# A decoder layer in float32: the value projection by PSUM bank, a hand-written order at the FFN entry, a norm's last phase held back, evictions first

## The chip, the cores and the metric

The kernel runs on one core of a Trainium2 chip. The time is device microseconds of one execution, lower is better. Matmuls run on TensorE (PE in the profile, PEld its weight loads), elementwise work on VectorE (DVE) and ScalarE (ACT), a little on GpSimd (POOL). Weights come by DMA from the queue of SyncE (SP). Each engine takes its own instructions in the order of the program, and waits for the others by semaphores.

## The reference, cut to what matters

One layer (DEPTH 1) over 256 tokens of 2048 channels, in float32. The four parts that the text speaks of are here:

```python
h = rms_norm(x, norm_mix_pre)
proj = h @ w_in          # 2048 columns in, split into a_in, b_in, q, kv, nsa_g, merge_g
y_a = conformer_conv(a_in, ...)          # GLU, causal depthwise conv (31 taps), layer norm, silu, projection
y_b = chunked_spatial_gating(b_in, ...)
y_c = native_sparse_attention(q, kv, nsa_g, ...)
g_a, g_b, g_c = split(sigmoid(merge_g), 3)
mixed = (g_a * y_a + g_b * y_b + g_c * y_c) @ w_o
x = x + rms_norm(mixed, norm_mix_post)
h = rms_norm(x, norm_ffn_pre)
u = causal_depthwise_conv(h @ w_up, ffn_conv_w, ffn_conv_b)      # 3 taps
u_g, u_v = split(u, 2)
x = x + rms_norm((silu(u_g) * u_v) @ w_down, norm_ffn_post)
```

The 256 tokens are handled as two halves of 128 (`t` is 0 or 1). `w_up` has 2 x 5632 columns.

## The kernel before

**Split weights.** A float32 product is made of three matmuls on rounded parts: every operand is split into a high half (rounded to the format that PE multiplies) and a low half (what is left). A weight piece of 128 x 1024 is fetched into `wraw` (5 buffers) by `fetch` (L96), ACT copies it to `whi` (L136), DVE subtracts to get `wlo` (L137); `whi` and `wlo` have 4 buffers each. This is `piece()`. Activations are kept in pairs too: `hT` (mixer input) and `h2` (FFN input, `h2T` in the trace) hold for each of 16 chunks `k` of 128 channels a high and a low half.

There are two shapes of matmul. `mm_t` (L185 to L187) keeps the activation still and moves the weights, three matmuls per chunk and token half. `lumps` (L165, L172) keeps a weight chunk still and moves the activation: one matmul of high weights against both halves of the activation (L165, 512 columns for 256 tokens), and one of low weights against the high half (L172, 256 columns). Its order is high, low, high.

**Order.** The program is written in one order, and a scheduler at build time arranges each engine's instructions by priority and by its own estimate. `tc.high_priority(offset)` puts an instruction ahead in its choice, `tc.issue_after(ins)` pins it behind another. `in_line` does that for PE: a run of matmuls behind the run before. Work beside the matmuls is written as generators in a queue `bg`. `pump(ns)` takes from the front of that queue as much nominal work as its budget says; `until(mark)` empties it to a mark. The budgets are BA, BB, BC and BG for the four stages of the mixer, BG = 2000 per call for the gated branches.

**The mixer.** After the first projections the convolution's generators (`conv_gen`, L419, result `cv`) run on DVE beside the matmuls of the later projections. Behind them in the queue stands `lna_gen`, the layer norm of the convolution: sums and squares (`lnm`, `lnv`), two matmuls that sum over partitions (L426), a square root, and a last phase of eight steps that applies it (`lz`, `lg`, L453 to L459, result `At`). Then come the compressed attention and the attention proper.

**The value projection** (`pvs`, 560 columns: 256 values, 48 gate logits, 256 values) loops over the 16 chunks; a piece has all 560 columns of one chunk, and for each chunk four accumulators (two token halves x columns 0 to 304 and 304 to 560) get three matmuls each. After the loop six evictions on ACT (L624 to L626) write `kkv` and `gsg`. The pool of accumulators (`acc`) has four buffers, and the next tile (`ps`, the query projection) takes the first one that is evicted.

**The gates.** `branch` (three branches x four column blocks) computes the gate `pg`, its tanh in four evictions on ACT (L819, `mg`), the branch projection `py`, and their product on DVE (L842, L845). The evictions have no raised priority.

**The FFN entry.** The output projection `po` ends with its last blocks done half by half, so that half 0 is normed while PE computes half 1. `done_o(cb, t)` takes the square on ACT (L894), the product with the norm's weights (L900), and for the last block the norm `norm1` (L279, L280, the square root L221, L222 to L225) and four residual additions (L903, 512 channels each). `enter2(t, k)` transposes one chunk (L909, `ptf`, four buffers) and splits it into `h2` (ACT L915, DVE L916). The first two tiles of the up projection (`pu`) are computed half by half:

```python
for f in range(2):
    for n, run in enumerate(lumps(pu2[f], ws2[f], h2, 0)):
        in_line(run)
        c = 3 * f + n - 2
        for k in range(4 * c, 4 * c + 4) if c >= 0 else ():
            in_line(enter2, 1, k)
for f in range(2):
    for run in lumps(pu2[f], ws2[f], h2, 1):
        in_line(run)
```

With `t` given, the low run has 16 matmuls of 128 columns per tile and half. `order2` pins the two instructions of an `enter2` behind those of the one before; the other instructions of ACT and DVE there are placed by the scheduler. Behind follow the third tile, the sum of squares of the residual (L993, L996), its norm, and 85 more tiles of the up projection.

Of the kernel before, what the change touches and what calls it, by code (L numbers as in the profile page):

```python
# [29 lines left out]
FF = 5632  # L30
NFT = FF // 128
EPS = 1e-6
BA, BB, BC, BG = 3000, 3000, 2500, 2000
PR = 1000
NW0, _ = 9, 6
S1, S2, S3 = 6, 12, 14
# [11 lines left out]
def block(ctx: ExitStack, tc: tile.TileContext, x, fp, cst, rows, sgw, w1, w2, wf_a, wt_bv, wf_bu, wf_c,  # L48
# [130 lines left out]
    def in_line(work, *args):  # L179

        with tc.issue_after(pe_last[0]):
            pe_last[0] = work(*args)

    def mm_t(ps, xh, xl, hi, lo, first, last):
        PE.matmul(ps, lhsT=xh, rhs=hi, start=first, stop=False)  # L185
        PE.matmul(ps, lhsT=xh, rhs=lo, start=False, stop=False)  # L186
        return PE.matmul(ps, lhsT=xl, rhs=hi, start=False, stop=last).ins  # L187
# [235 lines left out]
    def lna_gen():  # L423
        def total(acc, nm):
            ps = bank([128, T], "lnp" + nm)
            PE.matmul(ps, lhsT=ones, rhs=acc, start=True, stop=True)  # L426
            return ps
        acc = q1("lnm")
        V.tensor_add(acc, ca[:, 0], ca[:, 1])
        yield 345  # L430
        for j in range(2, 8):
            V.tensor_add(acc, acc, ca[:, j])
            yield 345
        mean = total(acc, "m")
# [12 lines left out]
        V.tensor_scalar(var, total(acc, "v"), EPS, None, op0=ALU.add)  # L447
        r = rsqrt(P1, var, T, "a")
        yield 3400
        for j in range(8):  # L450
            z = q1(f"lz{j}")
            g = q1(f"lg{j}")
            V.tensor_mul(ca[:, j], ca[:, j], r)  # L453
            S.activation(z, ca[:, j], AF.Identity, bias=fps[:, C_LB + j:C_LB + j + 1],
                         scale=fps[:, C_LG + j:C_LG + j + 1])
            S.activation(g, z, AF.Tanh, scale=0.5)
            V.scalar_tensor_tensor(z, g, 1.0, z, op0=ALU.add, op1=ALU.mult)
            S.activation(At[:, j, 0], z, AF.Copy, scale=0.5)
# [148 lines left out]
    for i in range(4):  # L607
# [5 lines left out]

    pvs = [[PS.tile([128, 304 if b == 0 else 256], F32, tag="acc", name=f"pvs{t}{b}") for b in range(2)]
           for t in range(2)]
    for k in range(KT):
        hi, lo = piece(wt_vs[:, k * 560:k * 560 + 560], 560)
        for t in range(2):
            ts = slice(t * 128, t * 128 + 128)
            for b, c in ((0, slice(0, 304)), (1, slice(304, 560))):  # L620
                mm_t(pvs[t][b], hT[:, k, 0, ts], hT[:, k, 1, ts], hi[:, c], lo[:, c], k == 0, k == KT - 1)
        pump(BUDGET * .25)
    for t in range(2):
        S.activation(vsw[:, t, 0:256], pvs[t][0][:, 0:256], AF.Copy, scale=r0[:, t:t + 1])  # L624
        S.activation(gsg[:, t], pvs[t][0][:, 256:304], AF.Tanh, scale=rh[:, t:t + 1])  # L625
        S.activation(vsw[:, t, 256:512], pvs[t][1], AF.Copy, scale=r0[:, t:t + 1])  # L626
    gsgf = gsg.rearrange("p t c -> p (t c)")
    V.tensor_scalar(gsgf, gsgf, 1.0, 0.5, op0=ALU.add, op1=ALU.mult)

# [171 lines left out]
    def branch(bi, act_of):  # L801

        for cb in range(4):
# [12 lines left out]
            for t in range(2):  # L816
                for a in range(2):
                    tgs[t, a] = q1(f"mg{bi}{cb}{t}{a}")
                    S.activation(tgs[t, a], pg[t][:, a * 256:a * 256 + 256], AF.Tanh, scale=rh[:, t:t + 1])  # L819
# [18 lines left out]
            for t in range(2):  # L838
                for a in range(2):
                    cc = slice(cb * 512 + a * 256, cb * 512 + a * 256 + 256)  # L840
                    y = mac[:, t, cc] if bi == 0 else tgs[t, a]
                    V.scalar_tensor_tensor(y, tgs[t, a], 1.0, py[t][:, a * 256:a * 256 + 256], op0=ALU.add,  # L842
                                           op1=ALU.mult)
                    if bi:
                        V.tensor_add(mac[:, t, cc], mac[:, t, cc], y)  # L845
            if bi == 2:
                bg.append(mix_gen(cb))
            pump(BUDGET)
# [43 lines left out]
    def done_o(cb, t):  # L892
        cc = slice(cb * 512, cb * 512 + 512)
        S.activation(junk, po[cb, t], AF.Square, accum_out=ss1[t][:, cb:cb + 1])  # L894
        if cb < 3:
            V.tensor_mul(y1[:, t, cc], po[cb, t], rw[:, cc])
            return
        with tc.high_priority():
            r1 = norm1(ss1[t], f"o{t}")
            V.tensor_mul(y1[:, t, cc], po[cb, t], rw[:, cc])  # L900
            for c in range(4):
                cc = slice(c * 512, c * 512 + 512)
                V.scalar_tensor_tensor(y1[:, t, cc], y1[:, t, cc], r1, x2[:, t, cc], op0=ALU.mult, op1=ALU.add)  # L903

    def enter2(t, k):

        pt = bank([128, 128], f"ptf{t}{k}")
        ts = slice(t * 128, t * 128 + 128)
        tr = PE.transpose(pt, y1[:, t, k * 128:k * 128 + 128], ident)  # L909
        w = fps[:, C_NFP + k:C_NFP + k + 1]  # L910
        with ExitStack() as order:
            order.enter_context(tc.high_priority())
            for ins in order2:
                order.enter_context(tc.issue_after(ins))
            a = S.activation(h2[:, k, 0, ts], pt, AF.Copy, scale=w)  # L915
            v = V.scalar_tensor_tensor(h2[:, k, 1, ts], pt, w, h2[:, k, 0, ts].bitcast(F32), op0=ALU.mult,  # L916
                                       op1=ALU.subtract)
        order2[:] = [a.ins, v.ins]
        return tr.ins

    order2 = []
# [26 lines left out]
    for n, (cb, p) in enumerate(HELD):  # L948
        for i in range(2):
            if n == 0 and i == 0:  # L950
                pe_last[0] = mm_o(cb, 1, p, held[n], (i,))
            else:
                in_line(mm_o, cb, 1, p, held[n], (i,))
            if (n, i) == (3, 1):
                h2 = P0.tile([128, KT, 2, T], R, tag="hT", name="h2T")
            k = 2 * n + i - 7
            for k in ([k] if 0 <= k < 14 else [14, 15] if k == 14 else []):
                in_line(enter2, 0, k)
                if k % 4 == 3:
                    behind.append(tuple(order2))  # L960
                    up = wf_up[k // 8][:, k // 4 % 2 * 1024:k // 4 % 2 * 1024 + 1024]
                    ws2[k // 8].append(piece(up, 1024))
        if p == 7:
            done_o(cb, 1)
    P1c.close()


# [6 lines left out]
    pu2 = [PS.tile([128, 2, T], F32, tag="acc", name=f"pu{f}") for f in range(2)]  # L974
    for f in range(2):
        for n, run in enumerate(lumps(pu2[f], ws2[f], h2, 0)):
            in_line(run)
            c = 3 * f + n - 2
            for k in range(4 * c, 4 * c + 4) if c >= 0 else ():
                in_line(enter2, 1, k)  # L980
    for f in range(2):
        for run in lumps(pu2[f], ws2[f], h2, 1):
            in_line(run)
    with ExitStack() as order:
        order.enter_context(tc.high_priority())
        for ins in order2:
# [106 lines left out]
def _layout(inp):  # L1093
# [31 lines left out]
    wt_vs = c(w_in[:, vs_cols].reshape(16, 128, 560).transpose(1, 0, 2)).reshape(128, 16 * 560)  # L1125
# [72 lines left out]
```

## Time and profile before

| | |
|---|---|
| runs | 1608.62, 1609.54, 1611.83 us; median 1609.54 |
| profiled execution | 1607.9 us, span 1606.2 us |
| granted clock of PE | 0.997 |
| PE busy | 1586.2 us (99%), 8293 matmuls |
| DVE, ACT busy | 1125.6 us (70%), 855.0 us (53%) |
| read from HBM | 299.13 MB, 188 GB/s over the span |

A row of the timeline has the start and the duration in us, the engine, the line, the operation, output and inputs, the shape, the count of merged instructions, and in brackets the idle time ahead with what ended it. Matmuls are pipelined and the profile models their ends, so that what one costs is read from the distance of starts, not from its duration. A row of the waits has who waited at which line for whom: total us, times, longest.

### The profile page before, as it was taken

What the parts mean: (1) busy time and instruction counts of PE and PEld (TensorE: products, weight loads), DVE (VectorE), ACT (ScalarE), POOL (GpSimd) and SP (SyncE); (2) the same over time, 40 slices, a digit from 0 to 9 for tenths busy, and PEclk for the clock granted to TensorE, in tenths of its full rate; (3) what the DMA queues carried; (4) which work ended last, traced back from release to release, by engine and by line L of the source; (5) the groups of instructions that cost most, each with busy time, mean ns of one, the idle gap of its engine ahead of it and who ended that gap; (6) DMA issues with size and microseconds to landing.
All of it is one profiled execution on the core that took longest, in us unless ns stands there. A gap on an engine that the chain in (4) does not pass through costs nothing.

```text
span 1606.2 us, 22284 instructions
## 1 busy us (share of the span) xinstructions
PE 1586.2 (99%) x8293; PEld 1346.7 (84%) x8293; DVE 1125.6 (70%) x1914; ACT 855.0 (53%) x1378; POOL 16.1 (1%) x45
## 2 busy tenths in 40 slices
PE   9999998999999999999999999999999999999997
PEld 7888887888887777788888888888888888888886
DVE  6799999887655555555558877777777777444444
ACT  6554444475466766444455655555555555344342
POOL 0000020000000000000000000000000000000000
PEclk9999999999999999999999999999999999999999
DMA  8655556557655455566773566666666666666663
GB/s 304 228 193 184 185 158 198 180 182 241 209 160 151 141 164 175 179 188 189 242 237 96 192 189 191 186 189 192 192 187 185 192 189 213 196 194 195 194 191 114
DMA packets 85438, 303.74 MB, mean 189 GB/s; under 512 B 9809, under 2 KB 10193, under 8 KB 84689
## 3 DMA queue, kind: packets, MB, share of 16 engines
q1 hardware_dynamic: 84096, 298.04, 58.6%
q0 software_dynamic: 944, 4.19, 0.7%
q8 instruction: 65, 1.06, 0.3%
q14 instruction: 45, 0.36, 0.1%
q10 hardware_dynamic: 288, 0.08, 0.0%
HBM read 299.13 MB, written 2.10 MB: 188 GB/s over the span
## 4 chain that ended last, share of the span: by engine, by line
PE 96%; DVE 2%; issue 0%; DMA 0%; ACT 0%; SPq 0%; DVEq 0%; ACTq 0%
PE ps L165 28%; PE ps L172 15%; PE po L186 7%; PE po L187 7%; PE po L185 7%; PE pg L185 5%; PE pg L187 5%; PE pg L186 5%; PE py L186 3%; PE py L187 3%; PE py L185 3%; DVE cv L419 1%; PE pv L185 1%; PE pv L186 1%; PE pv L187 1%; PE s L685 1%
## 5 line engine op out<-in xcount | busy, mean ns | idle before, releaser
L137 DVE TENSOR_TENSOR wlo<-wraw,whi 128x1024 fp32r<-128x1024 f32 (+1 forms) x533 | 644.7, 1212 | 301.6 <-ACT whi L136 294.1
L136 ACT ACTIVATE whi<-wraw 128x1024 fp32r<-128x1024 f32 (+1 forms) x533 | 554.9, 1045 | 368.9 <-PE po L187 135.7
L165 PE MATMUL ps<-h2T,whi 128*128 128x512 f32 x1360 | 324.6, 391 | 0.0
L165 PEld LDWEIGHTS ps<-h2T,whi 128*128 128x128 f32 x1360 | 250.0, 188 | 48.3
L172 PEld LDWEIGHTS ps<-h2T,wlo 128*128 128x128 f32 x1360 | 174.4, 191 | 6.6
L172 PE MATMUL ps<-h2T,wlo 128*128 128x256 f32 x1360 | 176.7, 283 | 0.0
L165 PE MATMUL ps<-hT,whi 128*128 128x512 f32 x640 | 158.3, 395 | 3.9 <-ACT gsg L625 3.9
L187 PE MATMUL pg<-whi,hT 128*128 128x512 f32 x384 | 151.0, 393 | 0.0
L186 PE MATMUL pg<-wlo,hT 128*128 128x512 f32 x384 | 150.1, 391 | 0.0
L185 PE MATMUL pg<-whi,hT 128*128 128x512 f32 x384 | 148.8, 394 | 0.0
L207 ACT ACTIVATE t<-ps 128x256 f32<-128x256 f32 x125 | 47.5, 382 | 173.8 <-PE ps L165 173.7
L165 PEld LDWEIGHTS ps<-hT,whi 128*128 128x128 f32 x640 | 117.6, 190 | 26.1 <-ACT gsg L625 4.1
L185 PE MATMUL po<-whi,gh 128*128 128x512 f32 x336 | 130.7, 389 | 0.0
L186 PE MATMUL po<-wlo,gh 128*128 128x512 f32 x336 | 130.7, 389 | 0.0
L187 PE MATMUL po<-whi,gl 128*128 128x512 f32 x336 | 130.7, 389 | 0.0
L208 DVE TENSOR_TENSOR t<-ps,t 128x256 f32<-128x256 f32 x125 | 53.1, 426 | 91.2 <-ACT t L207 91.1
L419 DVE SCALAR_TENSOR_TENSOR cv<-hb,fps,cv 128x256 f32<-128x256 f32 x240 | 106.8, 493 | 0.8 <-ACT cv L415 0.7
L172 PEld LDWEIGHTS ps<-hT,wlo 128*128 128x128 f32 x640 | 84.1, 191 | 4.3
L172 PE MATMUL ps<-hT,wlo 128*128 128x256 f32 x640 | 85.9, 283 | 0.0
L187 PEld LDWEIGHTS pg<-whi,hT 128*128 128x128 f32 x384 | 72.1, 188 | 15.4 <-issue 0.7
L185 PEld LDWEIGHTS pg<-whi,hT 128*128 128x128 f32 x384 | 71.9, 188 | 15.5 <-issue 1.5
L186 PEld LDWEIGHTS pg<-wlo,hT 128*128 128x128 f32 x384 | 72.1, 188 | 15.0 <-issue 0.3
(297 smaller groups left out, 1900.5 us busy)
## 6 DMA issues: line engine op xcount, KB each, us to landing
wraw<-in_wf_up_dram SPq DMA_DIRECT2D x176, 512.0 KB, 4.3
wraw<-in_wt_g_dram SPq DMA_DIRECT2D x96, 512.0 KB, 3.8
wraw<-in_wt_dn_dram SPq DMA_DIRECT2D x88, 512.0 KB, 4.4
wraw<-in_wt_p_dram SPq DMA_DIRECT2D x48, 512.0 KB, 3.9
wraw<-in_wf_a_dram SPq DMA_DIRECT2D x32, 512.0 KB, 4.6
wraw<-in_wt_o_dram SPq DMA_DIRECT2D x32, 512.0 KB, 4.5
wraw<-in_wt_bv_dram SPq DMA_DIRECT2D x16, 512.0 KB, 6.4
wraw<-in_wf_bu_dram SPq DMA_DIRECT2D x16, 512.0 KB, 4.4
```

Source lines behind the costliest of these rows:

```text
L136: S.activation(hi[:, :n], raw[:, :n], AF.Copy)
L137: V.tensor_sub(lo[:, :n], raw[:, :n], hi[:, :n].bitcast(F32))
L165: ins = PE.matmul(ps[:, :, ts], lhsT=ws[k // 8][0][:, c:c + 128], rhs=mov[:, k, :, ts], start=(k == 0 and not t), stop=(k == n - 1), skip_ ...
L172: ins = PE.matmul(ps[:, 1, ts], lhsT=ws[k // 8][1][:, c:c + 128], rhs=mov[:, k, 0, ts], start=False, stop=False, skip_group_check=True).ins
L185: PE.matmul(ps, lhsT=xh, rhs=hi, start=first, stop=False)
L186: PE.matmul(ps, lhsT=xh, rhs=lo, start=False, stop=False)
L187: return PE.matmul(ps, lhsT=xl, rhs=hi, start=False, stop=last).ins
L207: S.activation(t1, ps[:, 1], AF.Copy)
L208: V.tensor_add(t1 if rb is not None else dst, ps[:, 0], t1)
L419: V.scalar_tensor_tensor(ca[:, j], hb[:, j, k:k + T], w(j, k), ca[:, j], op0=ALU.mult, op1=ALU.add)
L685: last = PE.matmul(out, lhsT=lhsT, rhs=rhs, start=start, stop=stop, skip_group_check=True).ins
```

## The change

Five edits.

1. `wt_vs` is laid out by bank. The first 304 columns of all chunks come first, in six pieces of three chunks (912 columns; the last has one chunk, 304), then the other 256 columns in four pieces of four chunks (1024). The bank of 304 columns is computed for both halves and evicted, then the other. The evictions have raised priority.
2. The last phase of `lna_gen` yields until the mark `gates` is set, which is done once the first gate's tanh is written down.
3. The tanh of the gates and the products of gate and branch have raised priority.
4. BG is 2400 in place of 2000.
5. At the FFN entry ACT and DVE have an order written by hand from the fifteenth chunk of half 0 on (`fixed`). In it are the norm of half 1, the copy and the split of the last piece of the second tile's weights, the residuals between the transposes, and the split of the third tile's weights ahead of the sums of squares. The matmuls of the first two tiles have an order of their own, by quarters of the 16 chunks, and the low weights meet both halves at once (`up_lo`, 256 columns).

```diff
-BA, BB, BC, BG = 3000, 3000, 2500, 2000
+BA, BB, BC, BG = 3000, 3000, 2500, 2400
...
         r = rsqrt(P1, var, T, "a")
         yield 3400
+        while "gates" not in marks:
+            yield 2400
...
-    for k in range(KT):
-        hi, lo = piece(wt_vs[:, k * 560:k * 560 + 560], 560)
+    for b, (w, each, a0) in enumerate(((304, 3, 0), (256, 4, KT * 304))):
+        for k0 in range(0, KT, each):
+            ks = range(k0, min(k0 + each, KT))
+            hi, lo = piece(wt_vs[:, a0 + k0 * w:a0 + (ks[-1] + 1) * w], len(ks) * w)
+            for i, k in enumerate(ks):
+                c = slice(i * w, i * w + w)
+                for t in range(2):
+                    ts = slice(t * 128, t * 128 + 128)
+                    mm_t(pvs[t][b], hT[:, k, 0, ts], hT[:, k, 1, ts], hi[:, c], lo[:, c], k == 0, k == KT - 1)
+            pump(BUDGET * len(ks) * w / 2240)
         for t in range(2):
-            ts = slice(t * 128, t * 128 + 128)
-            for b, c in ((0, slice(0, 304)), (1, slice(304, 560))):
-                mm_t(pvs[t][b], hT[:, k, 0, ts], hT[:, k, 1, ts], hi[:, c], lo[:, c], k == 0, k == KT - 1)
-        pump(BUDGET * .25)
-    for t in range(2):
-        S.activation(vsw[:, t, 0:256], pvs[t][0][:, 0:256], AF.Copy, scale=r0[:, t:t + 1])
-        S.activation(gsg[:, t], pvs[t][0][:, 256:304], AF.Tanh, scale=rh[:, t:t + 1])
-        S.activation(vsw[:, t, 256:512], pvs[t][1], AF.Copy, scale=r0[:, t:t + 1])
+            with tc.high_priority(offset=int(PR)):
+                S.activation(vsw[:, t, b * 256:b * 256 + 256], pvs[t][b][:, 0:256], AF.Copy, scale=r0[:, t:t + 1])
+                if b == 0:
+                    S.activation(gsg[:, t], pvs[t][0][:, 256:304], AF.Tanh, scale=rh[:, t:t + 1])
...
-                    S.activation(tgs[t, a], pg[t][:, a * 256:a * 256 + 256], AF.Tanh, scale=rh[:, t:t + 1])
+                    with tc.high_priority(offset=int(PR)):
+                        S.activation(tgs[t, a], pg[t][:, a * 256:a * 256 + 256], AF.Tanh, scale=rh[:, t:t + 1])
+            marks.add("gates")
...
-                    V.scalar_tensor_tensor(y, tgs[t, a], 1.0, py[t][:, a * 256:a * 256 + 256], op0=ALU.add,
-                                           op1=ALU.mult)
-                    if bi:
-                        V.tensor_add(mac[:, t, cc], mac[:, t, cc], y)
+                    with tc.high_priority(offset=int(PR)):
+                        V.scalar_tensor_tensor(y, tgs[t, a], 1.0, py[t][:, a * 256:a * 256 + 256], op0=ALU.add,
+                                               op1=ALU.mult)
+                        if bi:
+                            V.tensor_add(mac[:, t, cc], mac[:, t, cc], y)
...
+    def fixed(eng, op, *args, **kw):
+        with ExitStack() as order:
+            order.enter_context(tc.high_priority())
+            for ins in seq.get(eng, ()):
+                order.enter_context(tc.issue_after(ins))
+            seq[eng] = [op(*args, **kw).ins]
...
+            if k == 14:
+                order_of(order2)
+                fixed(S, S.activation, junk, po[3, 1], AF.Square, accum_out=ss1[1][:, 3:4])
...
+    def up_hi(f, ks, t):
+        ts = slice(t * 128, t * 128 + 128)
+        for k in ks:
+            ins = PE.matmul(pu2[f][:, :, ts], lhsT=ws2[f][k // 8][0][:, k % 8 * 128:k % 8 * 128 + 128],
+                            rhs=h2[:, k, :, ts], start=(k == 0 and t == 0), stop=(k == KT - 1 and t == 1),
+                            skip_group_check=True).ins
+        return ins
+
+    def up_lo(f, ks):
+        for k in ks:
+            ins = PE.matmul(pu2[f][:, 1], lhsT=ws2[f][k // 8][1][:, k % 8 * 128:k % 8 * 128 + 128],
+                            rhs=h2[:, k, 0], start=False, stop=False, skip_group_check=True).ins
+        return ins
...
+    fixed(V, V.reduce_sum, v1, ss1[1], axis=AX.X)
+    fixed(V, V.tensor_scalar, v1, v1, 1.0 / D, EPS, op0=ALU.mult, op1=ALU.add)
+    fixed(S, S.activation, r1, v1, AF.Sqrt)
+    hi, lo = (P0.tile([128, 1024], R, tag=tag, bufs=4, name=tag + "last") for tag in ("whi", "wlo"))
+    fixed(S, S.activation, hi, raw, AF.Copy)
...
+    in_line(up_hi, 0, range(KT), 0)
+    in_line(up_hi, 1, range(12), 0)
+    for c in range(4):
+        if c == 0:
+            residual(0)
+            residual(1)
+        for k in quarter[c]:
+            in_line(enter2, 1, k)
+        if c == 0:
+            residual(2)
+            fixed(V, V.tensor_mul, y1[:, 1, 1536:], po[3, 1], rw[:, 1536:])
+            in_line(up_hi, 1, range(12, KT), 0)
+        elif c == 1:
+            residual(3)
+            fixed(V, V.tensor_sub, lo, raw, hi.bitcast(F32))
+        if c:
+            for f in range(2):
+                in_line(up_hi, f, quarter[c - 1], 1)
+        for f in range(2):
+            in_line(up_lo, f, quarter[c])
+    for f in range(2):
+        in_line(up_hi, f, quarter[3], 1)
...
+    raw = [fetch(wf_up[2][:, a:a + 1024], 1024) for a in (0, 1024)]
+    hs = []
+    for i in range(2):
+        hi, lo = (P0.tile([128, 1024], R, tag=tag, bufs=4, name=f"{tag}f2{i}") for tag in ("whi", "wlo"))
+        fixed(S, S.activation, hi, raw[i], AF.Copy)
+        fixed(V, V.tensor_sub, lo, raw[i], hi.bitcast(F32))
+        hs.append((hi, lo))
...
-    hs = granule(wf_up[2])
```

More of the change, by code (lines that the diff above doesn't have):

```diff
@@ L897, in done_o @@
             return
+        assert t == 0
         with tc.high_priority():
@@ L903, in done_o, with order_of @@
                 V.scalar_tensor_tensor(y1[:, t, cc], y1[:, t, cc], r1, x2[:, t, cc], op0=ALU.mult, op1=ALU.add)
+    seq = {}
+    def fixed(eng, op, *args, **kw):
[4 more added lines that the diff above has]
+            seq[eng] = [op(*args, **kw).ins]
+    def order_of(last):
+        seq[V] = seq[S] = list(last)
     def enter2(t, k):
@@ L910, in enter2 @@
         w = fps[:, C_NFP + k:C_NFP + k + 1]
[L911 to L918, printed above, removed]
+        if t == 0 and k < 14:
+            order_of(order2)
+        fixed(S, S.activation, h2[:, k, 0, ts], pt, AF.Copy, scale=w)
+        fixed(V, V.scalar_tensor_tensor, h2[:, k, 1, ts], pt, w, h2[:, k, 0, ts].bitcast(F32), op0=ALU.mult,
+              op1=ALU.subtract)
+        order2[:] = seq[S] + seq[V]
         return tr.ins
@@ L956, in block @@
             k = 2 * n + i - 7
+            if k == 14:
+                order_of(order2)
+                fixed(S, S.activation, junk, po[3, 1], AF.Square, accum_out=ss1[1][:, 3:4])
             for k in ([k] if 0 <= k < 14 else [14, 15] if k == 14 else []):
@@ L959, in block @@
                 if k % 4 == 3:
-                    behind.append(tuple(order2))
                     up = wf_up[k // 8][:, k // 4 % 2 * 1024:k // 4 % 2 * 1024 + 1024]
-                    ws2[k // 8].append(piece(up, 1024))
-        if p == 7:
-            done_o(cb, 1)
+                    if k < 15:
+                        behind.append(tuple(order2))
+                        ws2[k // 8].append(piece(up, 1024))
+                    else:
+                        raw = fetch(up, 1024)
+        if p == 7 and cb == 2:
+            done_o(cb, 1)
@@ new lines, in block @@
+    pu2 = [PS.tile([128, 2, T], F32, tag="acc", name=f"pu{f}") for f in range(2)]
+    def up_hi(f, ks, t):
[10 more added lines that the diff above has]
+        return ins
@@ new lines, in residual @@
+    def residual(c):
+        cc = slice(c * 512, c * 512 + 512)
+        fixed(V, V.scalar_tensor_tensor, y1[:, 1, cc], y1[:, 1, cc], r1, x2[:, 1, cc], op0=ALU.mult, op1=ALU.add)
+    v1 = PZ.tile([128, 1], F32, tag="ssv1", bufs=4, name="ssvo1")
+    r1 = PZ.tile([128, 1], F32, tag="rs_y1", bufs=2, name="rsyo1")
+    t1 = PZ.tile([128, 1], F32, tag="rs_t1", bufs=2, name="rsto1")
+    fixed(V, V.reduce_sum, v1, ss1[1], axis=AX.X)
+    fixed(V, V.tensor_scalar, v1, v1, 1.0 / D, EPS, op0=ALU.mult, op1=ALU.add)
@@ new lines, in block @@
+    fixed(S, S.activation, r1, v1, AF.Sqrt)
+    hi, lo = (P0.tile([128, 1024], R, tag=tag, bufs=4, name=tag + "last") for tag in ("whi", "wlo"))
+    fixed(S, S.activation, hi, raw, AF.Copy)
+    ws2[1].append((hi, lo))
+    fixed(V, V.reciprocal, r1, r1)
+    fixed(V, V.tensor_mul, t1, r1, r1)
+    fixed(V, V.scalar_tensor_tensor, t1, t1, -0.5, v1, op0=ALU.mult, op1=ALU.mult)
+    fixed(V, V.scalar_tensor_tensor, r1, t1, 1.5, r1, op0=ALU.add, op1=ALU.mult)
+    quarter = [range(4 * c, 4 * c + 4) for c in range(4)]
@@ L972, in block @@
     G.memset(ones2, 1.0)
[L974 to L983, printed above, removed]
+    raw = [fetch(wf_up[2][:, a:a + 1024], 1024) for a in (0, 1024)]
[5 more added lines that the diff above has]
+        hs.append((hi, lo))
     with ExitStack() as order:
         order.enter_context(tc.high_priority())
-        for ins in order2:
+        for ins in seq[V] + seq[S]:
             order.enter_context(tc.issue_after(ins))
@@ L1124, in _layout @@
     vs_cols = np.concatenate([kv + 768 + ar(256), n_cols, kv + 1280 + ar(256)])
-    wt_vs = c(w_in[:, vs_cols].reshape(16, 128, 560).transpose(1, 0, 2)).reshape(128, 16 * 560)
+    wt_vs = w_in[:, vs_cols].reshape(16, 128, 560).transpose(1, 0, 2)
+    wt_vs = np.concatenate([wt_vs[:, :, 0:304].reshape(128, -1), wt_vs[:, :, 304:].reshape(128, -1)], axis=1)
     up_cols = np.concatenate([np.concatenate([ar(128) + 128 * i, FF + ar(128) + 128 * i]) for i in range(NFT)])
```

## The prediction

> **What bounds the kernel now.** I read the page first, then TensorE's own waits, then the timelines around the two places where those waits stand.
>
> ```profile
> span 1606.2 us, 22284 instructions
> PE 1586.2 (99%) x8293; PEld 1346.7 (84%) x8293; DVE 1125.6 (70%) x1914; ACT 855.0 (53%) x1378; POOL 16.1 (1%) x45
> ```
>
> TensorE (PE) is busy for all but 20.0 us of the span. So a change that leaves the matmuls alone can win only those 20 us and the time that matmuls take beyond what they take elsewhere. The waits of PE name the places:
>
> ```profile
> PE ps L165 <- ACT gsg L625: 3.9, 1, 3.9
> PE pvs L186 <- DVE wlo L137: 2.4, 1, 2.4
> PE ptf L909 <- DVE y L903: 1.1, 1, 1.1
> PE ptf L909 <- DVE h2T L916: 0.6, 1, 0.6
> PE pvs L185 <- DVE t L208: 0.4, 1, 0.4
> ```
>
> Three of the five stand in the value projection (pvs, and the ps that follows it), two at the FFN entry (ptf). Those are the two stages whose order the change rewrites. A third part, the convolution norm and the gating evictions, lies where the windows show PE without a gap:
>
> ```profile
> 274.00:660.00 386.00, 386.00 (x1942) 313.84 (x1941) 247.62 (x507) 231.41 (x447) 1.65 (x9) 1.00 0.56 178
> ```
>
> (Columns: stretch and its length, then PE, PEld, DVE, ACT and POOL busy, granted clock, DMA.) In 386 us PE has no idle time, so nothing can be won there; VectorE (DVE) has 138.4 us spare, ScalarE (ACT) 154.6.
>
> **Value projection by bank.** Before, all four accumulators end at the same moment, and the next tile needs the first of their buffers. The timeline of that moment:
>
> ```profile
> 265.99 0.28 PE L187 MATMUL pvs<-whi,hT 128*128 128x256 f32 x1
> ...
> 268.47 1.06 ACT L136 ACTIVATE whi<-wraw 128x1024 fp32r<-128x1024 f32 x1 [2.18 <-DVE wlo L137]
> 269.44 0.46 ACT L624 ACTIVATE kkv<-pvs,rsyx 128x256 f32<-128x256 f32 x1
> ...
> 270.14 3.63 PE L165 MATMUL ps<-hT,whi 128*128 128x512 f32 x8 [3.87 <-ACT gsg L625]
> ...
> 273.60 1.12 PE L172 MATMUL ps<-hT,wlo 128*128 128x256 f32 x8
> ```
>
> And from the chain of work, further on, how fast such matmuls run undisturbed:
>
> ```profile
> 888.37 3.65 PE ps L165 x16
> ```
>
> The evictions stand on ACT behind a weight copy that itself waits until 268.47. PE stands for 3.9 us, and then its first eight 512-column matmuls take 3.46 us, from 270.14 to 273.60, where sixteen run in 3.65 elsewhere. That is another 3.46 - 1.83 = 1.6 us of slow matmuls right behind the stall. So the moment costs 3.9 + 1.6 = 5.5 us.
>
> After, the 304-wide bank of both halves is finished first, and its evictions run while the 256-wide bank is computed. In the changed program's order on ACT they stand ahead of the copy of the fourth 1024 piece. The second bank takes 96 matmuls of 256 columns. Sixteen of these take 1.91 us in 880.29 to 882.20 (quoted below), so 96 take 11.5 us. The four evictions, 0.46 us each at most, take 1.8. The next ps gets the first bank's buffer, free some 10 us before it is wanted. The tile after that wants bank two, evicted behind one more copy (1.06) and its own 0.46 at most, while PE has a 5.57 us tile to work on (3.65 + 1.91). So the 5.5 us go; the cover is the second bank, and without it they would return.
>
> The stall of 2.4 us has another cause:
>
> ```profile
> 234.22 0.76 DVE L137 TENSOR_TENSOR wlo<-wraw,whi 128x560 fp32r<-128x560 f32 x1
> ...
> 237.67 0.42 PE L185 MATMUL pvs<-whi,hT 128*128 128x304 f32 x2
> ...
> 240.04 0.30 PE L186 MATMUL pvs<-wlo,hT 128*128 128x304 f32 x1
> ...
> 240.17 0.30 PE L187 MATMUL pvs<-whi,hT 128*128 128x304 f32 x1
> ...
> 244.06 2.10 DVE L419 SCALAR_TENSOR_TENSOR cv<-hb,fps,cv 128x256 f32<-128x256 f32 x5
> ...
> 246.77 2.08 DVE L137 TENSOR_TENSOR wlo<-wraw,whi 128x560 fp32r<-128x560 f32 x3
> ...
> 265.28 1.27 DVE L137 TENSOR_TENSOR wlo<-wraw,whi 128x1024 fp32r<-128x1024 f32 x1
> ```
>
> DVE did eleven small operations in a row, five convolution steps (0.4 each) among them, between two low halves, and PE ran out. In the changed order on DVE there are ten pieces for sixteen, and at most seven small operations between two of them. I set each low half against its use. Ready: from 234.2, where DVE turns to the first piece in both orders, 0.4 per step, 0.34 per other small operation, and per split 1.0 (912 columns) to 1.15 (1024). Used: from 237.7, with 0.13 to 0.14 per 304-column matmul (240.04 to 240.17) and eighteen of them to a piece of 912. The fourth piece is ready near 243.8 and used near 245.2; the fifth near 246.3, used near 247.8; the first of the second bank near 250.4, used near 251.1. The last is the tightest, 0.7 us ahead. So 2.4 and the 0.4 go, if DVE keeps this pace. Sum of the stage: 5.5 + 2.4 + 0.4 = 8.3, and some 0.2 of restart, 8.5 us. Ends: 5.5 if DVE stays late; 9.1 by the whole stage, which lasts 35.9 us from 237.67 to 273.60, while its matmuls, 96 at 0.14, 96 at 0.12 and eight at 0.228, are 26.8.
>
> **FFN entry.** The rows of before on PE, then those of DVE, for which it waits:
>
> ```profile
> 858.86 0.38 PE L909 MATMUL ptf<-idn,y 128*128 128x128 f32 x2
> ...
> 860.03 1.90 PE L172 MATMUL pu<-h2T,wlo 128*128 128x128 f32 x16
> 861.77 1.17 PE L165 MATMUL pu<-h2T,whi 128*128 128x256 f32 x8
> 864.02 0.66 PE L909 MATMUL ptf<-idn,y 128*128 128x128 f32 x4 [1.09 <-DVE y L903]
> ...
> 866.27 1.10 PE L909 MATMUL ptf<-idn,y 128*128 128x128 f32 x4 [0.64 <-DVE h2T L916]
> ...
> 873.73 2.13 PE L165 MATMUL pu<-h2T,whi 128*128 128x256 f32 x16
> 875.70 1.90 PE L172 MATMUL pu<-h2T,wlo 128*128 128x128 f32 x16
> 877.44 3.01 PE L165 MATMUL pu<-h2T,whi 128*128 128x256 f32 x16
> 880.29 2.08 PE L172 MATMUL pu<-h2T,wlo 128*128 128x256 f32 x16
> 882.20 2.00 PE L165 MATMUL pu<-h2T,whi 128*128 128x512 f32 x8
> ```
>
> ```profile
> 843.78 0.14 DVE L280 TENSOR_SCALAR ssvo<-ssvo 128x1 f32<-128x1 f32 x1
> ...
> 844.98 2.74 DVE L903 SCALAR_TENSOR_TENSOR y<-y,rsyo,x 128x512 f32<-128x512 f32 x4
> ...
> 860.77 0.14 DVE L280 TENSOR_SCALAR ssvo<-ssvo 128x1 f32<-128x1 f32 x1
> ...
> 861.30 1.23 DVE L137 TENSOR_TENSOR wlo<-wraw,whi 128x1024 fp32r<-128x1024 f32 x1
> ...
> 863.22 2.74 DVE L903 SCALAR_TENSOR_TENSOR y<-y,rsyo,x 128x512 f32<-128x512 f32 x4
> ...
> 871.08 1.13 DVE L916 SCALAR_TENSOR_TENSOR h2T<-ptf,fps,h2T 128x128 fp32r<-128x128 f32 x4 [0.26 <-ACT h2T L915]
> ```
>
> *Fewer matmuls.* The low halves of the weights met the two token halves apart: 64 matmuls of 128 columns. They are now 32 of 256 columns. Sixteen of the narrow ones take 860.03 to 861.77, 1.74 us (0.109 each); sixteen of the wide ones 1.91 us (0.119 each). So 64 x 0.109 = 7.0 becomes 32 x 0.119 = 3.8: 3.1 us of PE's own work are gone.
>
> The Trainium skill speaks against this term: "TensorE: Matmul & The Clock Gate", section "Wait — 56ns, not 53.3ns?", has back-to-back warm matmuls start every N / 2.4 GHz + 2.5 ns, so that halving the columns would nearly halve the time. By that rule the merge would save some 0.1 us and the whole change 3 us less; the two rows do not follow it, since half the columns took 91% of the time.
>
> *The shorter chain.* The second half's norm goes from the mean (L280) to the first residual (L903). At the first half that took 843.78 to 844.98, 1.2 us. At the second it took 860.77 to 863.22, 2.45, because the split at 861.30 and its copy stood inside. After, that split is behind the third residual and inside the chain nothing is left but a copy on ACT behind the square root. With the mean near 860.9 the first residual starts near 862.1 and its transposes near 862.8, not 864.02. PE's 28 matmuls ahead of them, 0.123 each (sixteen in 873.73 to 875.70), end near 862.4, so it stands about 0.4 instead of 1.1.
>
> *What is late next.* Behind 862.8 PE has sixteen transposes (some 2.3 us), 36 high matmuls (4.4) and 32 low ones (3.8): 10.5, to 873.3. DVE from 862.1 has four residuals (2.74), a product (some 0.6), the moved split (1.2) and sixteen h2T (4 x 1.13): 9.1, to 871.2, and its last result is needed one microsecond before PE ends. They run almost level; a transpose of the third or fourth quarter waits until DVE has freed its bank, by some 0.4 us. The moved split would end near 869, about when PE comes to the second tile's low matmuls of the third quarter, which now wait for it. PE ends these tiles near 873.8. Before it was 878.4 (877.44 and eight of the sixteen at 0.123). Gain 4.6, I take 4.5; ends: 2.0, if DVE and not PE paces the quarters, and 5.5, if PE waits for nothing.
>
> Behind that nothing is late: the next tile's copies are first on ACT after the last h2T, and DVE has the remaining 21% of its time:
>
> ```profile
> 885.00:1372.00 487.00, 487.00 (x2785) 429.74 (x2784) 384.31 (x613) 281.13 (x440) 0.00 (x0) 1.00 0.62 191
> ```
>
> **The parts costed at nothing.** The norm's last phase now stands behind the first gating tanh, and tanh and gating products go ahead of weight splits. Neither removes work, and PE does not wait there now. The hold also stops the compressed-branch work queued behind it in the generator queue, and no DMA moves but the smaller number of value pieces on SP. The raised rate (2000 to 2400) hands that time back: in the changed order the last attention matmul on PE has some 15 us less of other matmuls ahead of it. Bounds: a gain of 0.5, a loss of 3, were two of the copies late by their own 1.06 plus a missed slot; I take 0.
>
> **Sum.** 8.5 + 4.5 = 13.0. The profiled execution took 1607.9; less 13.0 it is 1594.9. The median of the runs lies 1.6 above the profiled one (1609.54), so 1596.5.
>
> **Rivals.** *The entry gains nothing* (DVE's chain paces every quarter, and only the value stage wins): 1609.5 - 8.5 = 1601. Against it stands the arithmetic 9.1 against 10.5. Chance 0.10. *The merge saves nothing*, each matmul costing by its columns: 1596.5 + 3.1 = 1599.6. The two rows quoted speak against it. Chance 0.04. *New small waits in the gates* of 3 to 6 us in all: about 1601. Chance 0.10. *The stalls stay*, DVE again doing convolution steps ahead of splits and the entry's chain being late: within 0.2%. Chance 0.03.
>
> *Slower: the early evictions block ACT.* ACT works in order. A tanh put ahead of a weight copy waits for its gate's last matmul, and every copy behind it waits too.
>
> ```profile
> ACT mg L819 <- PE pg L187: 7.3, 7, 1.4
> ACT whi L136 <- PE pg L187: 102.1, 61, 4.8
> ```
>
> A piece feeds twelve matmuls, 2.73 us, and four pieces are held, so ACT may be held up by about 10.9 less a copy and a split (2.3), 8.6 us, before PE notices. Today's longest such wait is 1.4. There are twelve gating blocks; to end slower than now each would have to cost PE over 13.0 / 12 = 1.1 us, so a hold of nearly 10 us. At 2 us a block: 1596.5 + 24 = 1620.5. Copies wait for PE for 102.1 us in all, so ACT runs well ahead, which speaks against it. Chance 0.05.
>
> **How the numbers follow.** My forecast has 0.68. About 0.2%, 3.2 us, is what a measurement of this kernel can tell from no change. Faster: 0.68 + 0.10 + 0.04 + 0.10 = 0.92; same 0.03; slower 0.05. The low end is both upper bounds, 9.1 + 5.5 = 14.6, and the spread of the runs of 0.9: 1594.0, less the 0.5 of the gates, 1593.5. The high end takes in the first three rivals: 1602.5.
>
> **What would show it.** Right: PE's waits name neither gsg nor pvs; no stretch of half-speed ps matmuls behind the value stage; the low matmuls of pu are 48 rows of 256 columns; the value stage ends some 8 us earlier, and the first two up tiles 4 to 5 us more. Wrong: a wait of PE on wlo in the second value bank, ptf waits on h2T of more than 1 us in sum, or PE waits on whi in the gates, which would mean that the evictions block.

## The result, and the profile after

| | before | after |
|---|---|---|
| median of the runs | 1609.08 us (1607.12 to 1611.83) | 1594.33 us (1592.98 to 1594.54) |
| profiled execution, span | 1607.9, 1606.2 us | 1594.22, 1592.5 us |
| granted clock of PE | 0.997 | 0.998 |

The ratio is 0.9905, 95% interval 0.9888 to 0.9922: faster by 14.75 us between the medians. The forecast was 1596.5 us, range 1593.5 to 1602.5. The time fell within the range, and most of the steps hold. One step was wrong, and only the experiments show it: one of the edits that were costed at nothing, the hold, decides over the larger half of the gain.

The page of the changed kernel, and all of PE's waits in it (who waited at which line for whom: total us, times, longest):

```profile
span 1592.5 us, 22180 instructions
PE 1580.6 (99%) x8261; PEld 1343.1 (84%) x8261; DVE 1123.7 (71%) x1908; ACT 852.5 (54%) x1372; POOL 15.8 (1%) x45
```

```profile
PE pv L185 <- ACT swraw L107: 1.5, 1, 1.5
PE warm L266 <- POOL wz L263: 1.4, 1, 1.4
PE pth L292 <- DMA idn<-in_cst_dram: 0.2, 1, 0.2
```

All five waits of before that the prediction quoted are gone; what is left stands at the very start. There are 32 fewer matmuls.

*The value projection.* Timelines of ACT and of PE around the end of the first and of the second bank:

```profile
251.84 1.06 ACT L136 ACTIVATE whi<-wraw 128x1024 fp32r<-128x1024 f32 x1 [1.69 <-PE pvs L187]
252.81 0.46 ACT L630 ACTIVATE kkv<-pvs,rsyx 128x256 f32<-128x256 f32 x1
253.16 0.29 ACT L632 ACTIVATE gsg<-pvs,rh 128x48 f32<-128x48 f32 x1
...
265.42 0.84 ACT L630 ACTIVATE kkv<-pvs,rsyx 128x256 f32<-128x256 f32 x2 [1.46 <-PE pvs L187]
```

```profile
265.46 0.28 PE L187 MATMUL pvs<-whi,hT 128*128 128x256 f32 x1
265.58 2.08 PE L172 MATMUL ps<-hT,wlo 128*128 128x256 f32 x16
267.50 2.68 PE L165 MATMUL ps<-hT,whi 128*128 128x512 f32 x11
```

The first bank is evicted from 252.81 on, over 12 us before PE wants its buffer. The last pvs matmul starts at 265.46 and the next tile at 265.58. The sixteen ps matmuls behind it take 1.92 us (0.120 each), their full speed. From the first value matmul (238.85) to the first up matmul (850.98, below) it is 612.13 us; before, it was 858.99 - 237.67 = 621.32. That is 9.2 us less. In two other traces whose value stage is that of before (the experiments "FFN entry alone" and "Priority without the banks") this stretch is 620.66 and 620.61 us, and PE's wait on gsg 3.2 us in place of 3.9. So the stage is worth 8.5 to 9.2 us, by the execution that one compares with. DVE's timeline at the fourth low half, which the prediction had ready near 243.8:

```profile
243.92 1.10 DVE L137 TENSOR_TENSOR wlo<-wraw,whi 128x912 fp32r<-128x912 f32 x1
244.94 0.87 DVE L419 SCALAR_TENSOR_TENSOR cv<-hb,fps,cv 128x256 f32<-128x256 f32 x2
```

The next operation starts at 244.94, so it is ready by then. The stage begins 1.18 us later in this profile (238.85 against 237.67), so that is 243.8 on the time of before.

*The FFN entry.* PE and DVE (all instructions ordered by hand carry the helper's line, L923, or L932 on PE):

```profile
850.98 3.11 PE L1000 MATMUL pu<-h2T,whi 128*128 128x256 f32 x24
854.18 0.74 PE L1000 MATMUL pu<-h2T,whilast 128*128 128x256 f32 x4
854.80 0.66 PE L932 MATMUL ptf<-idn,y 128*128 128x128 f32 x4
855.22 0.72 PE L1000 MATMUL pu<-h2T,whilast 128*128 128x256 f32 x4
...
858.44 1.12 PE L1007 MATMUL pu<-h2T,wlo 128*128 128x256 f32 x8
859.40 0.60 PE L932 MATMUL ptf<-idn,y 128*128 128x128 f32 x4
859.76 1.20 PE L1000 MATMUL pu<-h2T,whi 128*128 128x256 f32 x8
...
870.66 1.52 PE L165 MATMUL ps<-h2T,whi 128*128 128x512 f32 x6
```

```profile
852.79 0.15 DVE L923 TENSOR_SCALAR ssvo<-ssvo 128x1 f32<-128x1 f32 x1
...
854.00 1.42 DVE L923 SCALAR_TENSOR_TENSOR y<-y,rsyo,x 128x512 f32<-128x512 f32 x2
...
862.47 1.13 DVE L923 SCALAR_TENSOR_TENSOR h2T<-ptf,fps,h2T 128x128 fp32r<-128x128 f32 x4 [0.64 <-ACT h2T L923]
```

From the first up matmul to the next tile it is 19.68 us (850.98 to 870.66). Before, it was 858.99 to 884.04, 25.05: 5.37 us less. The norm takes 1.21 us from the mean to the first residual (852.79 to 854.00), where it took 2.45.

9.2 + 5.4 = 14.6 us is what these two traces show. The two profiled spans differ by 13.7 only, because this execution reached its first value matmul 1.2 us later (238.85 against 237.67), and the tail behind the last matmul was 0.35 us shorter. Whether that start belongs to the change is not shown. Of the four runs of the changed kernel one has a span of 1591.3 us, the other three 1592.5 to 1592.8; what the ten traces say of it stands in the last section.

### The profile page after: what moved, and what is told of

The parts are those of the page before. It is cut to its first block, busy times and chain, and to the rows that moved or that the text cites. A ratio compares the mean times of both kernels' runs of the same rounds, so it can differ in the third digit from the quotient of the medians.

```text
span 1592.5 us, 22180 instructions
## 1 busy us (share of the span) xinstructions
PE 1580.6 (99%) x8261; PEld 1343.1 (84%) x8261; DVE 1123.7 (71%) x1908; ACT 852.5 (54%) x1372; POOL 15.8 (1%) x45
## 4 chain that ended last, share of the span: by engine, by line
PE 99%; DMA 0%; DVE 0%; ACT 0%; SPq 0%; DVEq 0%; issue 0%; ACTq 0%
PE ps L165 29%; PE ps L172 15%; PE po L187 7%; PE po L186 7%; PE po L185 7%; PE pg L185 6%; PE pg L186 6%; PE pg L187 6%; PE py L186 3%; PE py L187 3%; PE py L185 3%; PE pv L185 1%; PE pv L186 1%; PE pv L187 1%; PE s L691 1%; PE O L691 1%
## 5 line engine op out<-in xcount | busy, mean ns | idle before, releaser
L137 DVE TENSOR_TENSOR wlo<-wraw,whi 128x1024 fp32r<-128x1024 f32 x524 | 638.7, 1222 | 295.4 <-ACT whi L136 289.2
L136 ACT ACTIVATE whi<-wraw 128x1024 fp32r<-128x1024 f32 x524 | 550.0, 1054 | 365.5 <-PE po L187 135.7
```

The lines of the kernel that those rows point to most:

```text
L136: S.activation(hi[:, :n], raw[:, :n], AF.Copy)
L137: V.tensor_sub(lo[:, :n], raw[:, :n], hi[:, :n].bitcast(F32))
```

## The experiments

In all of them "before" is the kernel before, run on the same chip.

**The value projection alone.** The kernel before with edit 1 and nothing else.

```diff
 # before, plus
+for b, (w, each, a0) in enumerate(((304, 3, 0), (256, 4, KT * 304))):   # one bank, then the other
...
+            with tc.high_priority(offset=int(PR)):                      # evictions raised
```

> The kernel before with the value projection by bank and its raised evictions, and nothing else. Theory (each part wins in its own stage, and the parts add up): the stall behind gsg, the slow matmuls behind it and the stall behind wlo go, so the time falls by 8.5 to 9.2 us against the kernel before, ratio 0.9943 to 0.9947; first value matmul to first up matmul is 612 us in place of 621; the FFN entry keeps its 25.0 us from the first up matmul to the next tile's and its ptf wait of about 1.1 us. Rival (the gain needs the gates' edits, because an earlier start of the gates meets weight copies that are late): 3 us or less, with PE waits on whi in the gated branches. Rival (only the stall behind gsg goes): 5.5 us.

Measured: 1608.34 us against 1608.16, ratio 1.0002 (0.9993 to 1.0011). No gain at all. The stage itself won what it should: its last value matmul starts at 265.46, and no wait on gsg or wlo is left. But PE has a new wait, the longest in the kernel; PE's waits, its timeline there, ACT's, DVE's, and the window from 348 to 353 us (its last three columns: granted clock, DMA share, GB/s):

```profile
PE pg L185 <- ACT mg L823: 6.0, 1, 6.0
```

```profile
330.61 0.39 PE L185 MATMUL py<-whi,Bt 128*128 128x512 f32 x1
...
341.74 0.39 PE L187 MATMUL py<-whi,Bt 128*128 128x512 f32 x1
348.15 0.80 PE L185 MATMUL pg<-whi,hT 128*128 128x512 f32 x1 [6.02 <-ACT mg L823]
...
349.17 0.63 PE L187 MATMUL pg<-whi,hT 128*128 128x512 f32 x1
349.60 0.63 PE L185 MATMUL pg<-whi,hT 128*128 128x512 f32 x1
...
352.88 0.40 PE L187 MATMUL pg<-whi,hT 128*128 128x512 f32 x1
353.11 0.39 PE L185 MATMUL pg<-whi,hT 128*128 128x512 f32 x1
```

```profile
342.21 1.06 ACT L136 ACTIVATE whi<-wraw 128x1024 fp32r<-128x1024 f32 x1 [1.66 <-PE py L187]
343.18 0.58 ACT L454 ACTIVATE lz<-cv,fps 128x256 f32<-128x256 f32 x1
343.78 1.28 ACT L456 ACT_TABLE_LOAD   x1
345.07 0.42 ACT L456 ACTIVATE lg<-lz 128x256 f32<-128x256 f32 x1
...
347.28 1.55 ACT L823 ACTIVATE mg<-pg,rh 128x256 f32<-128x256 f32 x4
```

```profile
341.73 0.42 DVE L225 SCALAR_TENSOR_TENSOR rsya<-rsta,rsya 128x256 f32<-128x256 f32 x1
342.19 2.77 DVE L453 TENSOR_TENSOR cv<-cv,rsya 128x256 f32<-128x256 f32 x8
```

```profile
348.00:353.00 5.00, 4.85 (x12) 3.88 (x13) 3.84 (x12) 4.97 (x15) 0.51 (x4) 0.53 0.17 69
```

The first gate was complete when PE turned to py, at 330.61. Its tanh ran only at 347.28: three steps of the convolution norm's last phase (lz, lg) stand ahead of it on ACT, the first of them needs a product that DVE can only make behind the norm's root (rsya, 341.73), and a weight copy and a table load of 1.28 us come between. PE ended py at 341.97 (341.74 and one spacing of 0.23), wanted the gate's accumulator, and stood until 348.15: 6.2 us. Then eleven matmuls took 4.73 us (348.15 to 352.88) where 0.23 each (352.88 to 353.11) make 2.5: another 2.2, and the granted clock of that window is 0.53. Together that is 8.4 of the 8.5 to 9.2 us that the stage had won.

That could have been read in the trace of before. The same hand-over there, on ACT and on PE:

```profile
345.81 1.54 ACT L819 ACTIVATE mg<-pg,rh 128x256 f32<-128x256 f32 x4
```

```profile
339.06 0.39 PE L185 MATMUL py<-whi,Bt 128*128 128x512 f32 x1
...
349.94 0.39 PE L185 MATMUL pg<-whi,hT 128*128 128x512 f32 x1
```

The tanh was already 6.7 us behind its gate (339.06 to 345.81). In the experiment PE's next gate could start 0.87 us into the tanh (347.28 to 348.15), so before it could have started at 346.68. It was wanted at 349.94: a slack of 3.3 us. In the experiment PE arrives 8.0 us earlier (341.97; the stage won 9.2, and the start was 1.2 later), the tanh comes 1.5 us later, and 3.3 - 8.0 - 1.5 = -6.2, which is the stand.

**The gates' edits alone.** Edits 2, 3 and 4 on the kernel before.

```diff
+        while "gates" not in marks:
+            yield 2400
...
+                    with tc.high_priority(offset=int(PR)):   # gating tanh, and the products
...
-BA, BB, BC, BG = 3000, 3000, 2500, 2000
+BA, BB, BC, BG = 3000, 3000, 2500, 2400
```

> The kernel before with the raised rate of 2400, the norm's last phase behind the first gating tanh, and raised priority of the gating tanh and products, and nothing else. Theory: no change, within 0.5 us, since PE has no gap in these stages before. Rival (they feed the gates late or early): up to 3 us slower, with PE waits on whi, or 1 us or more faster, with shorter spacings of the 256-column matmuls there.

Measured: 1608.29 us against 1608.16, ratio 1.0000 (0.9991 to 1.0009). Alone, these edits are worth nothing that these runs can tell, as the theory said. So each of the two groups gives nothing by itself, and in the changed kernel, which has both, the 8.5 to 9.2 us of the value stage come through.

**The FFN entry alone.** Edit 5 on the kernel before.

```diff
 # before, plus
+            seq[eng] = [op(*args, **kw).ins]        # fixed(): ACT and DVE in a written order
...
+    def up_lo(f, ks):                               # low weights meet both halves at once
```

> The kernel before with the order by hand at the FFN entry, and nothing else. Theory (parts add up): 4.6 to 5.4 us less than the kernel before, ratio 0.9966 to 0.9971; first up matmul to the next tile's 19.7 us in place of 25.0; the value stage keeps its stalls of about 3.9 and 2.4 us. Rival (the entry only wins because the value stage is earlier, and DVE's chain paces the quarters otherwise): 2 us or less, with ptf waits on h2T.

Measured: 1601.97 us against 1608.16, ratio 0.9966 (0.9952 to 0.998). PE's waits (the two longest) keep those of the value stage, and none stands at the entry. Its timeline from the first up matmul to the next tile:

```profile
PE ps L165 <- ACT gsg L625: 3.2, 1, 3.2
PE pvs L186 <- DVE wlo L137: 2.4, 1, 2.4
```

```profile
858.22 3.10 PE L991 MATMUL pu<-h2T,whi 128*128 128x256 f32 x24
...
877.91 0.61 PE L165 MATMUL ps<-h2T,whi 128*128 128x512 f32 x2
```

19.69 us, as in the changed kernel. The entry wins its 5.4 us without the rest. The medians differ by 6.2; the interval is 3.2 to 7.7 us of 1608 and holds both.

**The hold taken back.** The changed kernel without edit 2.

```diff
-        while "gates" not in marks:
-            yield 2400
...
-            marks.add("gates")
```

> The changed kernel without the hold: the norm's last phase stands in the queue as before, while the rate of 2400, the raised priority of the gating tanh and products, the value projection by bank and the FFN entry stay. Theory (the hold is what lets the value stage's gain through: without it four steps of the norm's last phase stand on ACT ahead of the first gating tanh, which then waits for the norm's chain on DVE): PE waits some 6 to 7 us at the second gate for ACT's mg, then runs at half speed for some 4 us; 8 to 9.5 us are lost, so 1602 to 1604 us, ratio to the kernel before 0.995 to 0.997. Rival (the tanh's raised priority or the rate does it): 1594 to 1596 us, no such wait.

Measured: 1602.59 us against 1608.56, ratio 0.9965 (0.9953 to 0.9977). That is the gain of the FFN entry and no more. PE's wait is back, longer than in the first experiment, since here four steps of the norm stand ahead of the tanh:

```profile
PE pg L185 <- ACT mg L824: 7.0, 1, 7.0
```

The raised priority of the tanh was still there; it did not put the tanh ahead of those steps.

**The hold alone of the gates' edits.** Value projection, FFN entry and hold; the rate is 2000, tanh and products have their old priority.

```diff
-BA, BB, BC, BG = 3000, 3000, 2500, 2400
+BA, BB, BC, BG = 3000, 3000, 2500, 2000
...
-                    with tc.high_priority(offset=int(PR)):   # gating tanh, and the products
```

> The kernel before with the value projection by bank, the FFN entry and the hold alone: the rate stays 2000, and gating tanh and products keep their old priority. Theory (of the gates' edits only the hold matters): within 1 us of the changed kernel, 1593.5 to 1595.5 us, ratio 0.9900 to 0.9915, no PE wait in the gates. Rival (rate or priorities matter too): 2 us or more slower than the changed kernel, with a PE wait on mg or whi at a later gate.

Measured: 1593.46 us against 1608.56, ratio 0.9910 (0.9897 to 0.9924), the changed kernel's 0.9905 within the intervals. ACT's timeline at the first gate:

```profile
339.58 1.57 ACT L825 ACTIVATE mg<-pg,rh 128x256 f32<-128x256 f32 x4
...
341.97 0.61 ACT L456 ACTIVATE lz<-cv,fps 128x256 f32<-128x256 f32 x1
```

The tanh is ahead of the norm's last phase, and PE waits for nothing in the gates. Rate and raised priorities in the gates add nothing that these runs can tell.

**Priority without the banks.** The kernel before, by chunk as it was, with raised priority on the six evictions.

```diff
+    with tc.high_priority(offset=int(PR)):
         for t in range(2):
             S.activation(vsw[:, t, 0:256], pvs[t][0][:, 0:256], AF.Copy, scale=r0[:, t:t + 1])
...
```

> The kernel before with raised priority on the six evictions of the value projection, by chunk as before, and nothing else. Theory (what removes the stall is that one bank is complete early; an eviction cannot run before its accumulator is complete, and ACT still holds three copies that wait for wlo ahead of it): 0 to 1 us less than before, the stall behind gsg stays at 3 us or more. Rival (the evictions only stood behind copies, and priority is enough): about 5 us less, the stall at 1 us or under.

Measured: 1607.44 us against 1608.16, ratio 0.9999 (0.9990 to 1.0007). ACT's timeline:

```profile
265.30 1.06 ACT L136 ACTIVATE whi<-wraw 128x1024 fp32r<-128x1024 f32 x1 [1.92 <-DVE cv L419]
268.08 1.06 ACT L136 ACTIVATE whi<-wraw 128x1024 fp32r<-128x1024 f32 x1 [1.72 <-DMA wraw<-in_wf_q_dram]
269.04 0.46 ACT L625 ACTIVATE kkv<-pvs,rsyx 128x256 f32<-128x256 f32 x1
```

All six evictions now follow one another, but still behind a copy that starts at 268.08, and PE's wait on gsg is 3.2 us. The stall stays, as expected. The profile names another cause than I had put down: that copy waited for the DMA of its piece, where I had said wlo. But the queue of SyncE, which issues the fetches, was itself waiting for low halves (its waits from 245 to 272 us, and the low half in question on DVE):

```profile
SPq L96 <- DVE wlo L137: 21.5, 15, 4.4
```

```profile
261.22 0.76 DVE L137 TENSOR_TENSOR wlo<-wraw,whi 128x560 fp32r<-128x560 f32 x1
```

The fetch was issued at 262.01, 0.03 us behind the end of that low half, which freed its buffer, and took 6.0 us to land. So the low halves on DVE stand in the chain all the same, one step further up, with the 6.0 us of the fetch behind them.

**The banks without priority.** The changed kernel, its value evictions at their old priority.

```diff
-            with tc.high_priority(offset=int(PR)):           # the evictions of the value projection
```

> The changed kernel with the evictions of the value projection at their old priority, by bank as it is. Theory (the order by bank is what frees the buffer in time; the first bank is evicted while the second is computed, one weight copy earlier or later): within 0.5 us of the changed kernel, no wait on gsg or kkv. Rival (without priority an eviction stands behind a copy that waits for wlo): 1 to 4 us slower, with such a wait.

Measured: 1592.96 us against 1608.56, ratio 0.9907 (0.9893 to 0.9921), and no wait on gsg or kkv. The two experiments together: the new layout of the pieces is the whole of edit 1's effect, and its raised priority does nothing here. The layout changes two things, the order by bank and ten larger pieces for sixteen; no run has one without the other.

**The merge undone.** The changed kernel with the low weights against each half apart.

```diff
-            ins = PE.matmul(pu2[f][:, 1], ..., rhs=h2[:, k, 0], ...).ins
+            for ts in (slice(0, 128), slice(128, 256)):
+                ins = PE.matmul(pu2[f][:, 1, ts], ..., rhs=h2[:, k, 0, ts], ...).ins
```

> The changed kernel with the low weights of the first two up tiles again against each token half apart: 64 matmuls of 128 columns in place of 32 of 256, at the same places in the order. Theory (a matmul with its own weight load costs 0.109 us at 128 columns and 0.119 at 256): 64 x 0.109 - 32 x 0.119 = 3.1 to 3.2 us slower than the changed kernel, so about 1597.5; first up matmul to the next tile's 22.8 us in place of 19.7. Rival (the Trainium skill, TensorE: Matmul & The Clock Gate, section Wait - 56ns, not 53.3ns?: a matmul costs N / 2.4 GHz + 2.5 ns): 0.1 us slower. Rival (DVE's chain has slack to fill, so that added matmuls lie in a wait): 0 to 1 us.

Measured: 1597.41 us against 1608.56, ratio 0.9934 (0.9921 to 0.9946); PE's timeline:

```profile
851.44 0.36 PE L1000 MATMUL pu<-h2T,whi 128*128 128x256 f32 x1
...
856.24 1.90 PE L1008 MATMUL pu<-h2T,wlo 128*128 128x128 f32 x16
857.98 0.62 PE L932 MATMUL ptf<-idn,y 128*128 128x128 f32 x4
...
874.04 1.98 PE L165 MATMUL ps<-h2T,whi 128*128 128x512 f32 x8
```

From the first up matmul to the next tile it is 22.60 us, 2.92 more than with the merge. Sixteen narrow matmuls take 1.74 us (0.109 each), eight wide ones 0.96 in the changed kernel (858.44 to 859.40, 0.120 each). The rule of the Trainium skill ("TensorE: Matmul & The Clock Gate", section "Wait — 56ns, not 53.3ns?") would make this 0.1 us. It has no term for a weight load, and these matmuls, each of which has a weight load of its own, do not follow it.

## Why the prediction was right, and where its working was wrong

- **The value stage, 8.5 us:** it measured 9.2 against the profiled execution of before, at the upper end of 9.1, and 8.5 against the two other traces with the old value stage. The evictions and the splits came as laid out: the fourth piece was ready when it was said to be. The last addend, the 0.2 of restart, rests on no row. The three stalls and the slow matmuls make 8.3 us of the profiled execution, so the rest is 0.9 there; the stall on gsg alone differs by as much between executions (3.9 and 3.2 us). One reading is off, without effect on the sum: of the eleven small operations ahead of the late low half seven, not five, are convolution steps.
- **The parts costed at nothing:** this step was wrong. The sentences were "Neither removes work, and PE does not wait there now" and, for the bounds, "a gain of 0.5, a loss of 3". They are true of the kernel before, where these edits measured 0. They are false of the kernel in which the value stage is shorter: there the hold is worth some 9 us (1602.59 without it, 1594.33 with it by the medians, in separate sets of runs), and without it the change would have ended at the very top of the range (1602.5). I asked what is late next behind the FFN entry, and not behind the value stage. The forecast was right because the change contained the cure for a wait that I had not seen, and that is luck.
- **The rival "new small waits in the gates", 3 to 6 us:** the right place and the wrong form. It is one wait, 6.0 to 7.0 us and a slow restart, and it belongs to the kernel without the hold.
- **The FFN entry, 4.5 us:** it measured 5.4, near the upper end of 5.5, which was for PE waiting for nothing. PE's waits name nothing there; its starts show one short stop, ahead of the matmuls that need `whilast`, the copy that ACT makes behind the square root (853.09 to 854.13): 24 matmuls take 3.20 us (850.98 to 854.18), where at 0.123 each they would take 2.95. The merge was 2.9 for 3.1. The chain came as worked out: its 1.21 us, and the first residual 3.0 us behind the first up matmul (3.1 by the forecast). What was mis-sized is the rest, 2.45 for 1.4 (4.5 less 3.1). Four transposes take 0.36 to 0.42 us of PE (859.40 to 859.76; 854.80 to 855.22), where I had 2.3 / 4 = 0.58. And no transpose of the third or fourth quarter waited: DVE itself idled 0.64 us there.
- **The rival that the early evictions block ACT:** it did not come. ACT's tanh waited for its gate 7.9 us in all (7.3 before) and 1.4 at most (1.4 before), and no PE wait names whi.
- **The sum** was 13.0 us and 1594.9 for the profiled execution, which took 1594.22: the two short terms (1.6 us together) were mostly hidden by its later start. The 1.6 us that I added for the median were too much, since the median of after stands 0.1 us above its profiled execution; that is most of the 2.2 us between 1596.5 and 1594.33.

## What to carry to other kernels

When a stage is made shorter, list every hand-over downstream in the trace of before, with its slack: when the buffer was freed, and when PE wanted it. Here one had 3.3 us, behind a gain of 9. An edit that is worth nothing alone can be what lets another through, so price the parts in the kernel in which they will stand, and test each by taking it out of the full change as well as by adding it to the kernel before.

## What the runs showed of the hardware

- A long stand of PE cost more than its length: behind the 6.0 us stand ten matmuls of 512 columns started 0.43 us apart in place of 0.23, 2.2 us in all, and the granted clock was 0.53. The Trainium skill ("TensorE: Matmul & The Clock Gate", section "Wait — 56ns, not 53.3ns?") gives 426.7 ns for 512 columns while the array is cold, which the rows agree with. The 2.4 us stand of the kernel before did not: behind it the granted clock was 1.00 (247.60 to 252.00). Whether the length of the stand alone decides is not measured.
- The number of columns hardly sets the cost of a narrow matmul with its own weight load: 0.109 us at 128 columns, 0.120 at 256.
- The start differs by 0.8 to 1.9 us. In five of the ten traces the granted clock of the first 20 us is 0.91, and the first value matmul starts at 238.71 to 239.31; in the other five it is 1.00, and that matmul starts at 237.38 to 237.93. In the trace of after, matmuls of 512 columns start 0.43 us apart near 10 us (9.49 to 9.92), and 0.23 later. All five with the slow start have the value projection by bank, and of the five others only "The banks without priority" has it. So the change may make a slow start likelier; these runs do not settle it, and what tips it is open.
